# A hybrid decoder step on one core: moving one store and four PSUM copies between queues

## The chip, the core and the metric

The kernel runs on one core of one Trainium2 chip. The metric is the device time of one execution in microseconds; where several runs are shown, their median counts. The core has five engines with a queue each: PE (TensorE, matmuls; its weight loads are listed as PEld), DVE (VectorE), ACT (ScalarE), POOL (GpSimd) and SP (SyncE), which here issues most of the transfers. ACT's queue issues transfers too. An instruction that waits holds up whatever stands behind it on its engine.

## The reference

One layer of a decoder is computed in float32 for one prompt of 256 positions and for eight decoded sequences with one new token each, 264 columns in all. Cut to what matters here:

```python
def trunk_layer(x, attend, shift0, wkv0, lp):
    x = x + FFN_RES * swiglu(rmsnorm(x, n1), f1g, f1u, f1d)
    h = rmsnorm(x, nm)
    proj = h @ w_in
    q, k, v = ...                      # attention columns of proj
    o_att, k_buf, v_buf = attend(q, k, v, sinks)
    o_rwkv, shift, S = rwkv_time_mix(proj[..., ATT_COLS:], shift0, wkv0, ...)
    x = x + concat([o_att, o_rwkv]) @ w_out
    x = x + FFN_RES * swiglu(rmsnorm(x, n2), f2g, f2u, f2d)
    return x, k_buf, v_buf, S, shift

def rwkv_time_mix(proj, shift0, wkv0, ...):
    prev = concat([shift0[:, None], proj[:, :-1]], axis=1)
    xm = proj + mu * (prev - proj)     # r, k, v and three LoRA inputs are cut from xm
    ...
    def step(S, inp):                  # over the positions, for each of 16 heads of 64
        r_t, lw_t, k_t, v_t, kk_t, a_t = inp
        sa = einsum('bhij,bhj->bhi', S, -kk_t)
        S = (S * exp(lw_t)[:, :, None, :] + sa[..., None] * (kk_t * a_t)[:, :, None, :]
             + v_t[..., None] * k_t[:, :, None, :])
        return S, einsum('bhij,bhj->bhi', S, r_t)
    ...
    return out, proj[:, -1], S
```

The returned `proj[:, -1]` (the last projected row of the prompt and the row of each decoded token) is the shift state. It is one of the outputs.

## The kernel before

**Stages.** The first feed-forward block runs to about 780 us, the mixing stage (input projection, time mixing, attention, output projection) from there to about 1152 us, and the second feed-forward block to the end. All large matmuls go through `gemm` (lines 135 to 150 of the file): a weight block of 128x512 is loaded by SP into `raw`, split by ACT into `hi` (L132) and by DVE into `lo` (L59, a helper of all two-tensor operations), and each 128-column slice of it costs three matmuls (hi by hi, hi by lo, lo by hi) into a bank `acc` of PSUM. All matmuls that go through the helper `mm` have line 75; in `gemm` the name `big[0]` always holds the last matmul that was issued.

**The mixing stage.** `SEQ` lists the projected tiles: four batches `b`, then four `kv` tiles, then eight query tiles `q`. A batch has two pairs of heads (`BATCH = [2, 2, 2, 2]`), and for each pair three tiles are projected by `shifted`. `shifted` scales the tile (`pj`), and POOL copies its last nine columns to `shc` (L412); after the last of the 26 tiles `shc` holds the whole shift state.

**Tasks.** The work beside the projection is written as generators (`prep`, `chain`, `kvtask`, `attend`, `dec_scores`), advanced one step at a time by `tick` while `gemm` runs. This is the order in which the program is written down; a scheduler then puts the instructions of each engine into a list by their priorities and by a modelled time. `tc.high_priority()` lifts some of them, and `behind` ties an instruction in the scheduler to `big[0]`, without a semaphore on the chip.

**A batch's chain.** `chain(bt)` does, for the two pairs k = 0 and 1 of a batch: a triangular solve by DVE (30 steps of two operations, tiles `X`, `Xt` and `st`), whose inputs come back through DRAM by `Xt<-sa`; the second half of the inverse by small matmuls on `TT` and `W`, copied out by ACT (L600, L609); 16 matmuls for each pair, `m<-kr,TT`, into one PSUM bank each (`wus[k]`); from these banks the blocks `W[:, k]` (L622) and the two halves of `uv` (L626: half 0 by DVE, half 1 by ACT); then 24 matmuls for each pair on `W` (`m<-BT,W` and `m<-gm,W`), copied by L640 to `PT` and by DVE to `kr`; then the matmuls `m<-uv,BT` and `m<-gm,uv`; then the recurrence over the four chunks of 64 positions. L622 gives W's block of pair 0 to ACT and that of pair 1 to DVE:

```python
(A.copy, V.tensor_copy)[k % 2](W[:, k], v[:, 1:4, 0:64])
```

`W` is one tile of one buffer, filled by L600 and by L622 in turn. The tile pool tagged `m` has five PSUM banks for all these small products.

**The store of the shift state.** After the last batch has been spawned, L887 issues `A.dma_start(O["sh"], shc)` on ACT's queue: 117 KB, behind the copies of POOL into `shc`. Query tiles come later: for each, `win` projects it, DVE scales it into `ob[i]` (L62) and `attend` is spawned.

Of the kernel before, what the change touches and what calls it, by code (L numbers as in the profile page):

```python
# [26 lines left out]
BATCH = [2, 2, 2, 2]  # L27
# [20 lines left out]
def body(tc, I, O):  # L48
    nc = tc.nc
    V, A, G, TE, SP = nc.vector, nc.scalar, nc.gpsimd, nc.tensor, nc.sync  # L50
# [7 lines left out]
    def tt(e, out, a, b, op):  # L58
        return e.tensor_tensor(out=out, in0=a, in1=b, op=op)  # L59
# [14 lines left out]
    def mm(out, lhsT, rhs, start=True, stop=True, **k):  # L74
        return TE.matmul(out, lhsT, rhs, start=start, stop=stop, **k)  # L75

    def behind(i):
        tc.add_manual_dep(i.ins, big[0].ins.name, mybir.DependencyInfo(mybir.DependencyClass.NoSync, mybir.DependencyReason.SCHED_ONLY))
        return i
# [12 lines left out]
    def spawn(g):  # L92
        tasks.append(g)
        return g

    def pause(n):
        for _ in range(n):
            yield

    with ExitStack() as ctx:  # L100
# [14 lines left out]
        def tmp(shape=(P, T), dt=F32):  # L115
            pool, n = cur[0]
            return pool.tile(list(shape), dt, tag="t", bufs=n, name=uid("t"))
# [4 lines left out]
        def mp():  # L122
            return pp.tile([P, 512], F32, tag="m", bufs=NM, name=uid("m"))
# [42 lines left out]
        def vc(i):  # L166
            return vec[:, i:i + 1]
# [189 lines left out]
        def mixing_body(mx, n2, n3, XD, XR):  # L357
            def fix(shape, name):
                return mx.tile(list(shape), F32, name=name)

            def ring(shape, tag, bufs):
                return mx.tile(list(shape), F32, tag=tag, bufs=bufs, name=uid(tag))

            def load(src, shape):
                t = ring(shape, "ld", NLD)
                SP.dma_start(t, src)
                return t
# [6 lines left out]
            shc = fix((P, NSH, NB + 1), "shc")  # L374
# [24 lines left out]
            def win(t):  # L399
                ps = acc()  # L400
                gemm(ps, I["win"][t], n2.xs, tick)
                if not have[0]:
                    n2.rstd(rs)
                    have[0] = True
                return ps
# [137 lines left out]
            def newbatch(i):  # L543
                bt = Batch()
                n = BATCH[i]
                bt.i, bt.n, bt.left, bt.p0, bt.near = i, n, n, sum(BATCH[:i]), 0
                bt.KR, bt.bv = [None] * n, [None] * n
                bt.Gm = [[None, None] for _ in range(n)]
                bt.BT = [None] * n
                bt.UV = ring((P, 4, n, P), "uv", NUV)  # L550
                return bt

            def chain(bt):
# [27 lines left out]
                W, PT = ring((P, n, 3, 64), "W", 1), ring((P, n, 3, 64), "PT", 1)  # L581
# [37 lines left out]
                            mm(wus[k][r, c * P:c * P + P], TT[r, k * 4 + c, :], bt.KR[k][r, 0:3:2, c, :])  # L619
                for k in range(n):  # L620
                    v = wus[k].rearrange("p (c t) -> p c t", c=4)
                    (A.copy, V.tensor_copy)[k % 2](W[:, k], v[:, 1:4, 0:64])  # L622
                for k in range(n):
                    v = wus[k].rearrange("p (c t) -> p c t", c=4)
                    for h in range(2):
# [12 lines left out]
                for k in range(n):  # L638
                    v = pbs[k][:, :384].rearrange("p (c t) -> p c t", c=3)
# [104 lines left out]
            def softmax(s, mxv, sinks, n):  # L744
                nm, sm, es = (ring((P, 4), "st" + x, 6) for x in "abc")
                ts(V, nm[:, :n], mxv[:, :n], -1.0, ALU.mult)
                for j in range(n):
                    act(s[j], s[j], AF.Exp, bias=nm[:, j:j + 1], accum_out=sm[:, j:j + 1])
                w = n // len(sinks)
                for h, x in enumerate(sinks):  # L750
                    act(es[:, h * w:(h + 1) * w], nm[:, h * w:(h + 1) * w], AF.Exp, bias=x)
                tt(V, sm[:, :n], sm[:, :n], es[:, :n], ALU.add)
                V.reciprocal(sm[:, :n], sm[:, :n])
                for j in range(n):
                    if j < 2:
                        ts(V, s[j], s[j], sm[:, j:j + 1], ALU.mult)
                    else:
                        act(s[j], s[j], AF.Copy, scale=sm[:, j:j + 1])

            def attend(t, q):  # L760
                p = t // 4
                G.tensor_copy(qd[:, p, :, t % 4], q[:, NP:T])
                bs = [load(I["bias"][(2 * p + h) * 4 + t % 4], (P, 256)) for h in range(2)]
                yield
                spp = [mp(), mp()]
                for h in range(2):
                    mm(spp[h][:, 0:256], q[:, P:NP], kT[p][h][:, 0:NP])
                    mm(spp[h][:, 256:384], q[:, 0:P], kT[p][h][:, 0:P])
                sc = [(tmp((P, 256)), tmp((P, P))) for h in range(2)]
                mxv = ring((P, 4), "mxv", 6)  # L770
                for h, sps in enumerate(spp):
                    s1, s0 = sc[h]
                    head = (2 * p + h) * 4 + t % 4
                    for s, a, b, j in ((s1, sps[:, 0:256], bs[h], 0), (s0, sps[:, 256:384], bs[h][:, P:256], 1)):
                        V.tensor_tensor_reduce(out=s, in0=a, in1=b, op0=ALU.add, op1=ALU.max, scale=1.0,
                                               scalar=vc(VSK + head), accum_out=mxv[:, 2 * h + j:2 * h + j + 1])
                softmax([x for y in sc for x in y], mxv, [vc(VSK + (2 * p + h) * 4 + t % 4) for h in range(2)], 4)
                yield
                yield from pause(PW[4])
                for s1, s0 in sc:  # L780
                    tp = mp()
                    TE.transpose(tp[:, 0:P], s0, ident)  # L782
                    TE.transpose(tp[:, P:2 * P], s1[:, 0:P], ident)
                    TE.transpose(tp[:, 2 * P:3 * P], s1[:, P:256], ident)
                    A.copy(s1, tp[:, 0:256])
                    V.tensor_copy(s0, tp[:, 256:384])
                yield
                pt = sc
                op = mp()
                for h in range(2):  # L790
                    mm(op[:, h * 256:h * 256 + 256], Vt[p][:, 0, :], pt[h][0], True, False)
                    mm(op[:, h * 256 + P:h * 256 + 256], Vt[p][:, 1, :], pt[h][1], False, True)
                for h in range(2):
                    A.copy(q[HALF[h], :NP], op[HALF[h], h * 256:h * 256 + 256])
                mixed[8 + t] = q
# [80 lines left out]
            bat, att, bts, scores = [], [], [], []  # L876
            for kind, i in SEQ:
                if kind == "b":
                    bt = newbatch(i)
                    for k in range(BATCH[i]):  # L880
                        p = bt.p0 + k
                        x = [shifted(2 + 3 * p + j, tmp()) for j in range(3)]
                        spawn(prep(p, bt, k, *x))
                    bat.append(spawn(chain(bt)))
                    bts.append(bt)
                    if len(bat) == len(BATCH):
                        A.dma_start(O["sh"], shc)  # L887
                elif kind == "kv":
                    w, p = i // 2, i % 2
                    ps = win(LKV + i)  # L890
                    if w:
                        xs = (tmp(),)
                        with tc.high_priority():
                            tt(V, xs[0], ps[:, :T], rs, ALU.mult)
                    else:
                        xs = (kvb[2 * p], kvb[2 * p + 1])
                        kT[p] = xs
                        for h in range(2):
                            G.memset(xs[h][HALF[1 - h], :], 0.0)
                            with tc.high_priority():  # L900
                                tt(V, xs[h][HALF[h], :], ps[HALF[h], :T], rs[HALF[h], :], ALU.mult)
                    spawn(kvtask(w, p, xs))
                else:
                    ps = win(LKV + 4 + i)
                    q = ob[i]
                    with tc.high_priority():
                        stt(q, ps[:, :T], 0.125, rs, ALU.mult, ALU.mult)
                    att.append(spawn(attend(i, q)))
                    if i % 4 == 3:
                        scores.append(spawn(dec_scores(i // 4)))  # L910
                    if len(att) == 8:
                        att.append(spawn(dec_attend(list(att), scores)))
# [201 lines left out]
```

## Time and profile before

| | us |
|---|---|
| median of 3 runs | 1961.34 |
| lowest and highest | 1960.53, 1962.97 |
| the profiled execution, whole | 1958.83 |
| the profiled execution, its span | 1957.0 |
| PE idle in the stretch 780 to 1152 us | 6.16 |

The span goes from the first to the last instruction; the whole time has a little more at both ends. In what follows, a row of a timeline has the start (us from the span's start), the length, the engine, the line of the kernel, the operation and the tiles (written <- read), and in brackets how long the engine was idle before it and what released it. A row of a list of waits has the total us, the number and the longest. The chain of waits is the work that ended last, followed back from the last instruction. "ACTq" and "SPq" are DMA issues on those queues.

### The profile page before, as it was taken

To read this page: it belongs to the slowest core of one execution; us is meant where nothing else is said; L and a number is where in the kernel's file an instruction comes from. 1 tells how busy PE (TensorE), PEld (TensorE's weight loads), DVE (VectorE), ACT (ScalarE), POOL (GpSimd) and SP (SyncE) were. 2 spreads that over 40 slices of the span, in tenths; PEclk is the share of its full clock that TensorE was granted. 3 is DMA by queue.
4 is the path that set the end of the run, shared out by engine and by line. 5 is a ranking of instruction groups with operands and counts; after the bars stand their busy time and mean duration, and the time that the engine had idled before them with its cause. 6 is when DMAs were issued, how large, how long until landed. Compare 5 with 4: busy or idle time off the path is not lost.

```text
span 1957.0 us, 45229 instructions
## 1 busy us (share of the span) xinstructions
PE 1940.1 (99%) x17011; PEld 1922.1 (98%) x17011; DVE 1313.1 (67%) x2591; ACT 1036.4 (53%) x2069; POOL 264.1 (13%) x382
## 2 busy tenths in 40 slices
PE   9999999999999999999999999999999999999998
PEld 9999999999999999999889999999999999999998
DVE  5865555655556567799988766766666666666665
ACT  5644444444444456665556755654444444444445
POOL 0401001010010122232210000210101001010012
PEclk9999999999999999999999999999999999999999
DMA  7666666666656567555455455566666666666654
GB/s 241 178 194 194 186 194 196 184 189 178 188 183 185 184 194 230 165 162 153 136 151 167 137 157 185 176 187 188 191 189 193 188 194 191 191 195 183 195 182 148
DMA packets 218875, 357.26 MB, mean 183 GB/s; under 512 B 33552, under 2 KB 72352, under 8 KB 218656
## 3 DMA queue, kind: packets, MB, share of 16 engines
q1 hardware_dynamic: 212144, 345.76, 59.4%
q10 hardware_dynamic: 6512, 8.61, 1.4%
q8 instruction: 133, 2.18, 0.4%
q14 instruction: 86, 0.70, 0.1%
HBM read 346.67 MB, written 9.69 MB: 182 GB/s over the span
## 4 chain that ended last, share of the span: by engine, by line
PE 95%; DVE 3%; DMA 1%; issue 1%; ACT 1%; SPq 0%; DVEq 0%; POOL 0%; ACTq 0%
PE acc L75 87%; PE m L75 7%; DVE lo L59 1%; DVE Xt L59 0%; DVE st L59 0%; DMA Xt<-sa 0%; DMA x<-in_x 0%; DMA raw<-in_win 0%; DVE y L59 0%; SPq L564 0%; DVE gm L59 0%; ACT t L69 0%; DMA sa<-gm 0%; PE m L782 0%; ACT BT L521 0%
## 5 line engine op out<-in xcount | busy, mean ns | idle before, releaser
L59 DVE TENSOR_TENSOR lo<-raw,hi 128x512 fp32r<-128x512 f32 (+1 forms) x1288 | 874.5, 683 | 511.0 <-ACT hi L132 489.8
L132 ACT CAST hi<-raw 128x512 fp32r<-128x512 f32 (+1 forms) x1288 | 777.0, 606 | 822.0 <-PE acc L75 741.5
L75 PE MATMUL acc<-x,hi 128*128 128x264 f32 x5034 | 932.7, 286 | 2.2 <-DVE o L62 1.2
L75 PEld LDWEIGHTS acc<-x,hi 128*128 128x128 f32 x5034 | 781.4, 189 | 5.8 <-ACT hi L132 2.4
L75 PE MATMUL acc<-x,lo 128*128 128x264 f32 x2517 | 719.8, 286 | 0.5 <-DVE lo L59 0.5
L75 PE MATMUL acc<-h,hi 128*128 128x264 f32 x2752 | 495.0, 284 | 0.0
L75 PEld LDWEIGHTS acc<-x,lo 128*128 128x128 f32 x2517 | 475.5, 189 | 2.9 <-DVE lo L59 1.3
L75 PEld LDWEIGHTS acc<-h,hi 128*128 128x128 f32 x2752 | 424.4, 189 | 0.0
L75 PE MATMUL acc<-h,lo 128*128 128x264 f32 x1376 | 387.8, 284 | 0.0
L75 PEld LDWEIGHTS acc<-h,lo 128*128 128x128 f32 x1376 | 259.2, 189 | 0.0
L59 POOL TENSOR_TENSOR t<-t,t 128x264 f32<-128x264 f32 x74 | 80.3, 1085 | 1095.9 <-DVE t L59 949.7
L75 PE MATMUL acc<-y,hi 128*128 128x264 f32 x648 | 122.7, 284 | 0.0
L75 PE MATMUL acc<-o,hi 128*128 128x264 f32 x648 | 120.1, 284 | 0.0
L75 PE MATMUL acc<-kv,hi 128*128 128x264 f32 x582 | 109.2, 284 | 0.0
L75 PEld LDWEIGHTS acc<-y,hi 128*128 128x128 f32 x648 | 101.2, 189 | 0.1
L75 PEld LDWEIGHTS acc<-o,hi 128*128 128x128 f32 x648 | 100.1, 189 | 0.0
L62 DVE SCALAR_TENSOR_TENSOR x<-acc,x 128x264 f32<-128x264 f32 x192 | 81.2, 427 | 24.5 <-PE acc L75 23.6
L75 PE MATMUL acc<-y,lo 128*128 128x264 f32 x324 | 92.0, 284 | 0.0
L75 PE MATMUL acc<-o,lo 128*128 128x264 f32 x324 | 92.0, 284 | 0.0
L75 PEld LDWEIGHTS acc<-kv,hi 128*128 128x128 f32 x582 | 90.0, 189 | 0.0
L59 DVE TENSOR_TENSOR t<-acc,t 128x264 f32<-128x264 f32 x156 | 67.4, 432 | 32.8 <-PE acc L75 32.8
L75 PE MATMUL acc<-kv,lo 128*128 128x264 f32 x291 | 82.7, 284 | 0.0
(280 smaller groups left out, 1534.9 us busy)
## 6 DMA issues: line engine op xcount, KB each, us to landing
raw<-in_gu SPq DMA_DIRECT2D x688, 256.0 KB, 3.4
raw<-in_dn SPq DMA_DIRECT2D x224, 256.0 KB, 2.9
raw<-in_win SPq DMA_DIRECT2D x152, 256.0 KB, 3.4
raw<-in_dn SPq DMA_DIRECT2D x160, 192.0 KB, 2.7
raw<-in_wout SPq DMA_DIRECT2D x64, 256.0 KB, 3.3
xsp<-x ACTq DMA_DIRECT2D x16, 132.0 KB, 3.6
x<-xsp SPq DMA_DIRECT2D x16, 132.0 KB, 4.0
ld<-in_sT SPq DMA_DIRECT2D x16, 128.0 KB, 3.7
```

What stands on the lines that cost most here:

```text
L59: return e.tensor_tensor(out=out, in0=a, in1=b, op=op)
L62: return V.scalar_tensor_tensor(out=out, in0=a, scalar=s, in1=b, op0=op0, op1=op1)
L75: return TE.matmul(out, lhsT, rhs, start=start, stop=stop, **k)
L132: A.copy(hi[:, :w], raw[:, :w])
```

## The change

Two edits. L622 uses ACT for both pairs. The store of the shift state is taken out of the branch of the batches and issued after query tile 1 has been projected and its `attend` spawned; it is put through `behind`, so that the scheduler places it after the last matmul of that tile's projection. It stays on ACT's queue.

```diff
@@ -619,7 +619,7 @@
                 for k in range(n):
                     v = wus[k].rearrange("p (c t) -> p c t", c=4)
-                    (A.copy, V.tensor_copy)[k % 2](W[:, k], v[:, 1:4, 0:64])
+                    A.copy(W[:, k], v[:, 1:4, 0:64])
@@ -883,8 +883,6 @@
                     bat.append(spawn(chain(bt)))
                     bts.append(bt)
-                    if len(bat) == len(BATCH):
-                        A.dma_start(O["sh"], shc)
                 elif kind == "kv":
@@ -906,6 +904,8 @@
                     att.append(spawn(attend(i, q)))
+                    if i == 1:
+                        behind(A.dma_start(O["sh"], shc))
                     if i % 4 == 3:
```

## The prediction

> **What bounds the kernel now.** I read the page first, then the busy times by stage, then who PE waited for in the mixing stage, and only then the chain of waits and the rows of all engines around those waits.
>
> ```profile
> span 1957.0 us, 45229 instructions
> PE 1940.1 (99%) x17011; PEld 1922.1 (98%) x17011; DVE 1313.1 (67%) x2591; ACT 1036.4 (53%) x2069; POOL 264.1 (13%) x382
> 780.00:1152.00 372.00, 365.84 (x3924) 349.21 (x3923) 308.26 (x868) 235.70 (x622) 66.04 (x152) 1.00 0.54 152
> ```
>
> PE is the bound over the whole execution. The edit sits in the mixing stage, about 780 to 1152 us (third row: length of the stretch, then busy us of PE, PEld, DVE, ACT and POOL, granted clock, DMA share, GB/s). There PE is idle for 372.00 - 365.84 = 6.16 us. An edit that shortens no PE work, as this one, can give back about that much at most: 0.31% of the time. What PE waited for there, and what ACT waited for (total us, times, longest):
>
> ```profile
> PE m L75 <- ACT TT L609: 1.5, 1, 1.5
> PE m L75 <- DVE W L622: 1.3, 2, 0.9
> ...
> ACT hi L132 <- PE acc L75: 61.9, 62, 3.1
> ...
> ACT TT L609 <- POOL shc L412: 3.8, 1, 3.8
> ...
> ACT uv L626 <- DVE uv L626: 3.2, 1, 3.2
> ```
>
> The first two rows are the places that the edit touches: 1.5 + 1.3 = 2.8 us of PE. The question is whether PE keeps these 2.8 us or waits again a few instructions later. The row with shc is the store: L609 stands behind it in ACT's queue, and the store waits for the last copy into shc.
>
> **The store.** It is one DMA on ACT's queue. Here is its surrounding in time order (start, length, engine, line; idle time before it in brackets), in batch 1, the second of four:
>
> ```profile
> 950.62 0.19 DVE L59 TENSOR_TENSOR st<-X,Xt 128x30 f32<-128x30 f32 x1 [1.68 <-DMA Xt<-sa]
> 953.03 0.68 POOL L412 COPY shc<-pj 128x9 f32<-128x9 f32 x1 [4.38 <-DVE pj L59]
> 953.75 0.35 ACTq L887 DMA_DIRECT2D out_sh<-shc  x1
> 954.14 0.75 ACT L609 COPY TT<-m 32x256 f32<-32x256 f32 x2 [3.83 <-POOL shc L412]
> 954.55 2.35 PE L75 MATMUL m<-kr,TT 64*64 64x128 f32 x32 [1.46 <-ACT TT L609]
> 956.11 0.32 ACT L622 COPY W<-m 128x192 f32<-128x192 f32 x1
> 958.34 0.41 DVE L626 COPY uv<-m 64x256 f32<-64x256 f32 x1
> 958.49 0.33 PE L75 MATMUL m<-BT,W 64*64 64x64 f32 x4
> 959.39 0.34 DVE L622 COPY W<-m 128x192 f32<-128x192 f32 x1
> 959.66 0.41 DVE L626 COPY uv<-m 64x256 f32<-64x256 f32 x1
> 959.79 0.33 PE L75 MATMUL m<-BT,W 64*64 64x64 f32 x4 [0.38 <-DVE W L622]
> 960.10 0.37 ACT L626 COPY uv<-m 64x256 f32<-64x256 f32 x1
> 960.63 1.15 PE L75 MATMUL m<-uv,BT 128*64 128x64 f32 x32
> ```
>
> Without the store in front, ACT can do L609 3.83 us sooner, and PE starts the 32 matmuls m<-kr,TT 1.46 us sooner, at 953.09. In an unchanged order everything of PE behind them moves up by 1.46, and the matmuls on W start at 958.49 - 1.46 = 957.03. They need 0.91 us for each pair (958.49 to 959.40, the second start less its wait of 0.38), so they would end near 958.85. Next in PE's queue come the matmuls on uv, and uv's second pair is written by DVE and then ACT. What is late next is therefore DVE's uv, and DVE does not care for the store: from 950.62 to 959.66 it runs without a wait through the triangular solve of the next batch. The chain that ended last says the same. It does not pass through the store:
>
> ```profile
> 946.49 4.04 DMA Xt<-sa
> ...
> 958.42 0.33 DVE uv L626
> 958.75 0.60 DVE bk L59
> ...
> 959.47 0.28 DVE W L622
> ...
> 959.79 2.93 PE m L75 x88
> ```
>
> The chain lies on DVE before 959.79, and further back it goes to the transfer Xt<-sa. So in an unchanged order the store alone gives PE 1.46 us at 953 and takes it back at 959: **0** is the value I take for it alone. Its bounds are 0 and -1.46.
>
> At its new place the store comes behind the last matmul of query tile 1, by a tie for the scheduler only, with no semaphore on PE. shc has been complete since 953.71 (953.03 + 0.68), so it waits for nothing there. It costs ACT's queue the 0.35 of its row; the gap before the W copy of batch 2 (0.94, below) is larger. The transfer passes the small stores of keys and values on the same queue; none of them has a reader in the kernel:
>
> ```profile
> out_kp<-kv ACTq DMA_DIRECT2D x4, 32.0 KB, 3.3
> ...
> out_sh<-shc ACTq DMA_DIRECT2D x1, 117.0 KB
> ```
>
> Those are four stores each for kp and vp, and 117 KB beside a stage that moves 152 GB/s x 372 us = 56.5 MB. Value 0; if the cover of ACT's gap is gone, 0.35 on ACT.
>
> **The W copies.** Four copies (one in each batch) leave DVE and go to ACT:
>
> ```profile
> L622 ACT COPY W<-m x4: 319/319/319, 887.1 to 1070.1; 128x192 f32<-128x192 f32 x4
> L622 DVE COPY W<-m x4: 327/347/351, 888.3 to 1069.9; 128x192 f32<-128x192 f32 x4
> ```
>
> DVE sheds 4 x 0.347 = 1.39 us, ACT takes 4 x 0.319 = 1.28 us. The same bytes move, so PE's matmuls are unchanged.
>
> [...]
>
> *Batch 1.* W's second block would be ready on ACT by 956.11 + 0.64 = 956.75, before the 957.03 computed above, so the wait of 0.38 goes. DVE's second uv starts at 959.39 in place of 959.66, 0.27 sooner. ACT's uv follows it 0.44 later (959.66 to 960.10), so it ends near 959.39 + 0.44 + 0.37 = 960.20, and PE starts on uv at about 960.35 with a handoff of 0.15 as an estimate (959.79 less the end of the W copy, 959.73, is 0.06; a little more is left for ACT's queue). Against 960.63 that is **-0.28**. Here the edit as a whole removes 1.46 + 0.38 = 1.84 us of waits and gets 0.28.
>
> *Batch 2.* The same copies, at query tile 1:
>
> ```profile
> 1020.10 0.32 ACT L622 COPY W<-m 128x192 f32<-128x192 f32 x1 [0.94 <-PE m L75]
> ...
> 1023.59 0.37 ACT L626 COPY uv<-m 64x256 f32<-64x256 f32 x1 [3.17 <-DVE uv L626]
> 1023.88 0.35 DVE L622 COPY W<-m 128x192 f32<-128x192 f32 x1
> 1024.28 0.20 PEld L75 LDWEIGHTS m<-BT,W 64*64 64x64 f32 x4 [1.03 <-DVE W L622]
> 1024.62 0.37 ACT L626 COPY uv<-m 64x256 f32<-64x256 f32 x1
> 1025.13 1.15 PE L75 MATMUL m<-uv,BT 128*64 128x64 f32 x32
> ```
>
> ACT is idle for 3.17 us behind its first W copy, so the second costs nothing there. PE's W wait (0.89 on PE, 1.03 on the weight load) goes, and PE then waits for ACT's second uv, which ends at 1024.99: at once only 0.1 is gained. DVE, however, is 0.35 ahead from here on, and it holds the path to the next PE wait. I take the DVE copy's length, **-0.35**; bounds 0 and -0.89.
>
> *Batches 0 and 3.* PE does not wait for W there, so there is no wait to remove. In batch 3 ACT runs without a gap from its W copy to its second uv, and that uv is what PE's next matmuls need:
>
> ```profile
> 1070.12 0.32 ACT L622 COPY W<-m 128x192 f32<-128x192 f32 x1
> 1070.33 0.80 ACT L69 ACTIVATE t<-t,stb 128x256 f32<-128x256 f32 x2
> ...
> 1072.73 0.37 ACT L626 COPY uv<-m 64x256 f32<-64x256 f32 x1
> 1072.96 1.28 PE L75 MATMUL m<-uv,BT 128*64 128x64 f32 x31
> ```
>
> One more copy ahead of it makes it later by 0.21 (1070.12 to 1070.33, the step from one to the next) to 0.32: **+0.21**. In batch 0 I take 0: what else stands between is work that PE does anyhow.
>
> Behind an added ACT copy queue the casts hi<-raw, which feed every matmul. Their cover is the 61.9 us in which the casts themselves wait for PE to free a buffer (62 times, 1.0 us on average): 0.32 is inside that. Without this cover all 1.28 would be on PE.
>
> **Sum.** 0 - 0.28 - 0.35 + 0.21 = -0.42 us. The profiled execution took 1958.83 us, 1.83 more than its span of 1957.0, and the runs shown have a median of 1961.34, 2.51 above it. Span 1957.0 - 0.42 = 1956.6; on the median **1960.9**. Unknown is what a new list order does: the whole program is scheduled again behind the first moved copy at 887, and no row shows that. From the rows, its bounds are -6.16 (all PE idle of the stage) and, on the other side, the blocked queues below.
>
> **Rivals.** *All removed waits are kept.* The new order puts gemm matmuls between W and uv, or DVE's uv ahead of solve steps, so that nothing else becomes late: 1.46 + 1.27 (0.38 + 0.89), and DVE's 1.39 on its path to PE as well: -4.1, 1957.2 us. For it: the last chain lies on DVE at both places. Against: the DVE queue is without a gap there, and W copies are only two of its many steps.
>
> *Slower: ACT blocked behind DVE's uv.* In batch 2 ACT stood idle 3.17 us for DVE's uv, and the store's 3.83 us cost PE 1.46; so from 3.83 - 1.46 = 2.4 us of a blocked ACT on, each further us is one of PE. With both W copies early on ACT and uv late on DVE, ACT could stand before uv for 3.8 us in three more batches: 3 x 1.46 = 4.4, with no gain from the rest: 1965.7 us. For it: DVE is that late in batches 1 and 2. Against: the list of ACT's waits, quoted above, has that wait once in four batches.
>
> *It does nothing.* Both gains are taken back by the next DVE wait and batch 3's cost stays: 0 to +0.2, 1961.4 us.
>
> **How the numbers follow.** Changes within 0.2%, 3.9 us, can't be told from no change here. Forecast 0.45, nothing 0.15, all kept 0.20, blocked 0.20. The first two are inside the bound, the third is faster, the fourth slower: faster 0.2, same 0.6, slower 0.2. The likeliest is 1960.9, with its own range from -2.7 to +1.0 for the order, 1958.6 to 1962.3. The whole range reaches to the two others and slightly short of all PE idle: 1956.8 to 1965.7.
>
> **What would show it.** Right: no ACT wait for POOL shc at L609; PE's matmuls on TT start sooner behind the gemm of the last projected tile; no PE wait for DVE W; a new or longer PE wait for uv (ACT or DVE L626) in batches 1 and 2; PE idle of the stage between 5 and 6.2 us. Wrong: PE idle below 3 us (the gain was kept), or ACT waits of over 2.4 us in front of L626 with PE idle above 9 us. If the order of PE's gemm and batch matmuls is another one, the sum holds only by its bounds.

## The result, and the profile after

The changed kernel takes 1969.57 us (median of 6 runs, 1966.69 to 1974.05) against 1960.42 us for the kernel before (1959.19 to 1962.97, 6 runs): a ratio of 1.0054, 95% interval 1.0044 to 1.0064. It is slower by 9.15 us, where 1960.9 us was forecast, and it lies beyond the upper end of the range, 1965.7. The profiled execution took 1971.91 us, 1.8 more than its span.

From the page and from the busy times by stage of the changed kernel (PE, PEld, DVE, ACT, POOL, then granted clock, DMA share, GB/s):

```profile
span 1970.1 us, 45231 instructions
PE 1947.6 (99%) x17011; PEld 1929.0 (98%) x17011; DVE 1315.6 (67%) x2587; ACT 1040.2 (53%) x2075; POOL 263.3 (13%) x382
...
780.00:1152.00 372.00, 359.64 (x3849) 342.79 (x3847) 305.46 (x850) 235.00 (x612) 64.42 (x149) 0.99 0.53 150
```

The first thing to see is that PE is idle for 372.00 - 359.64 = 12.36 us in the mixing stage, where it was 6.16. The second is PE's busy total: as many matmuls as before take 7.5 us longer, and the granted clock of the stage is 0.99 where it was 1.00. Idle and clock together are the 13.1 us by which this span is longer: 6.2 us more of idle time, and the slices of 20 us that were granted less than full clock (a slice at 0.91 loses 9% of 20 us, 1.8 us; the kernel before has no slice below 1.00 between 780 and 1160 us):

```profile
960.00:980.00 20.00, 19.79 (x233) 18.45 (x234) 18.77 (x68) 10.20 (x28) 4.74 (x10) 0.91 0.41 112
1020.00:1040.00 20.00, 16.93 (x247) 15.67 (x247) 18.51 (x75) 5.67 (x14) 0.95 (x4) 0.91 0.36 101
1140.00:1160.00 20.00, 19.23 (x132) 18.66 (x131) 9.20 (x27) 6.53 (x19) 1.13 (x3) 0.83 0.36 110
```

1.8 + 1.8 + 3.4 = 7.0 us, so 6.2 + 7.0 = 13.2. This execution lies 2.3 us above the median of its kernel; the share of the clock differs from run to run: the mean granted clock of the six runs goes from 0.993 to 0.997.

What PE waited for (total us, times, longest) in the stage and up to 1215 us:

```profile
PE m L75 <- ACT W L622: 4.8, 2, 3.1
PE acc L75 <- DVE o L62: 2.6, 1, 2.6
PE m L75 <- ACT t L69: 1.4, 1, 1.4
```

The waits for ACT's TT (1.5) and for DVE's W (1.3) are gone, as the change intends. In their place PE waits 4.8 us for the W copies on ACT, and 1.4 us for an activation t on ACT, which is a new wait. The wait for the query eviction o (DVE's scaling of a finished query tile, which it reads from PSUM) has grown to 2.6 from the row of the kernel before:

```profile
PE acc L75 <- DVE o L62: 1.2, 1, 1.2
```

The rows of all engines around the first of these (start, length, engine, line; idle time before it in brackets) show what stands between the two W copies of batch 1:

```profile
954.03 1.96 PE L75 MATMUL m<-kr,TT 64*64 64x128 f32 x32
955.23 0.32 ACT L622 COPY W<-m 128x192 f32<-128x192 f32 x1 [2.00 <-PE m L75]
...
959.35 0.61 ACT L69 ACTIVATE t<-t,less,half 128x264 f32<-128x264 f32 x1 [3.80 <-DVE t L62]
...
959.86 0.30 ACT L622 COPY W<-m 128x192 f32<-128x192 f32 x1
960.21 0.33 PE L75 MATMUL m<-BT,W 64*64 64x64 f32 x4 [1.69 <-ACT W L622]
...
1026.71 0.37 ACT L626 COPY uv<-m 64x256 f32<-64x256 f32 x1 [5.28 <-DVE uv L626]
1027.10 0.32 ACT L622 COPY W<-m 128x192 f32<-128x192 f32 x1
1027.47 0.33 PE L75 MATMUL m<-BT,W 64*64 64x64 f32 x4 [3.07 <-ACT W L622]
```

The second copy does not follow the first. In batch 1 (954 to 960 us) an activation that waits 3.80 us for DVE stands in between, in batch 2 a uv copy that waits 5.28 us for DVE. That looks like the whole cause: ACT blocked behind DVE, as in the slower rival. The experiments say that it is not.

### The profile page after: what moved, and what is told of

Its sections match the earlier page's. It is cut to its first block, busy times and chain, and to the rows that moved or that the text cites. A ratio compares the mean times of both kernels' runs of the same rounds, so it can differ in the third digit from the quotient of the medians.

```text
span 1970.1 us, 45231 instructions
## 1 busy us (share of the span) xinstructions
PE 1947.6 (99%) x17011; PEld 1929.0 (98%) x17011; DVE 1315.6 (67%) x2587; ACT 1040.2 (53%) x2075; POOL 263.3 (13%) x382
## 4 chain that ended last, share of the span: by engine, by line
PE 94%; DVE 2%; DMA 1%; ACT 1%; issue 1%; SPq 0%; ACTq 0%; DVEq 0%; POOL 0%
PE acc L75 86%; PE m L75 7%; DVE lo L59 1%; DMA Xt<-sa 0%; DMA sa<-gm 0%; DVE st L59 0%; DVE Xt L59 0%; DMA x<-in_xT 0%; DMA ld<-in_cv 0%; DVE y L59 0%; ACT t L69 0%; SPq L564 0%; DVE t L716 0%; DVE gm L59 0%; ACT L69 0%
## 5 line engine op out<-in xcount | busy, mean ns | idle before, releaser
L75 PE MATMUL acc<-x,hi 128*128 128x264 f32 x5034 | 933.0, 286 | 4.0 <-DVE o L62 2.6
L75 PEld LDWEIGHTS acc<-x,hi 128*128 128x128 f32 x5034 | 782.9, 189 | 7.6 <-issue 3.1
L75 PE MATMUL acc<-x,lo 128*128 128x264 f32 x2517 | 721.8, 287 | 1.0 <-DVE lo L59 1.0
L75 PE MATMUL acc<-h,hi 128*128 128x264 f32 x2752 | 495.0, 284 | 0.0
L75 PEld LDWEIGHTS acc<-x,lo 128*128 128x128 f32 x2517 | 476.5, 189 | 3.7 <-DVE lo L59 1.8
L75 PEld LDWEIGHTS acc<-h,hi 128*128 128x128 f32 x2752 | 424.4, 189 | 0.0
L75 PE MATMUL acc<-h,lo 128*128 128x264 f32 x1376 | 387.9, 284 | 0.0
L75 PEld LDWEIGHTS acc<-h,lo 128*128 128x128 f32 x1376 | 259.2, 189 | 0.0
L75 PE MATMUL acc<-y,hi 128*128 128x264 f32 x648 | 122.7, 284 | 0.0
L75 PE MATMUL acc<-o,hi 128*128 128x264 f32 x648 | 120.1, 284 | 0.0
L75 PE MATMUL acc<-kv,hi 128*128 128x264 f32 x582 | 109.2, 284 | 0.0
L75 PEld LDWEIGHTS acc<-y,hi 128*128 128x128 f32 x648 | 101.2, 189 | 0.1
L75 PEld LDWEIGHTS acc<-o,hi 128*128 128x128 f32 x648 | 100.1, 189 | 0.0
L75 PE MATMUL acc<-o,lo 128*128 128x264 f32 x324 | 92.0, 284 | 0.0
L75 PE MATMUL acc<-y,lo 128*128 128x264 f32 x324 | 92.0, 284 | 0.0
L75 PEld LDWEIGHTS acc<-kv,hi 128*128 128x128 f32 x582 | 90.0, 189 | 0.0
L75 PE MATMUL acc<-kv,lo 128*128 128x264 f32 x291 | 82.7, 284 | 0.0
```

## The experiments

Each run is set against runs of the kernel before on the same chip. The edits are shown shortened. In the kernels with held lists the line numbers are 12 higher (L75 is L87 there).

**Which edit.** First each edit alone:

```
e1_wcopy   -  (A.copy, V.tensor_copy)[k % 2](W[:, k], v[:, 1:4, 0:64])
           +  A.copy(W[:, k], v[:, 1:4, 0:64])
e2_store   -  if len(bat) == len(BATCH): A.dma_start(O["sh"], shc)
           +  if i == 1: behind(A.dma_start(O["sh"], shc))
```

> The W edit alone: L622 on ACT for both pairs, the store where it was before. Theory A (ACT's queue order: the second W copy stands behind an ACT instruction that waits for DVE, L69 in batch 1 and L626 in batch 2, and PE idles for it): nearly the whole loss is here, 1967 to 1971 us, PE waits for ACT W L622 of about 3 us and 1.7 us less what the store's block of ACT covers. Theory B (the moved store is what hurts, by another order behind it): within 2 us of the kernel before, and no PE wait for ACT W over 1 us.

> The store edit alone: the store behind query tile 1, L622 on ACT and DVE in turn as before. Theory A: within 2 us of the kernel before (1958.5 to 1962.5), the wait of ACT TT for POOL shc gone, and a PE wait for DVE W or uv in batch 1 that has grown by about what was saved. Theory B: 1967 us or more.

The W copies alone: 1969.1 us, ratio 1.0050 [1.0035, 1.0065]. The store alone: 1961.8 us, 1.0009 [0.9999, 1.0018]. So the loss comes with the copies. The store's own row shows how its gain is lost; who PE waited for in e2_store:

```profile
PE m L75 <- DVE W L622: 2.3, 1, 2.3
```

The 1.46 us for TT are gone, and the wait for DVE's W in batch 1 has grown to 2.3: a little more than the 1.46 + 0.38 of before. DVE was on the path behind the store all along.

**Is it the place in ACT's queue?** Two kernels let the second W copy come ahead of what blocked it. In e3_tie_uv the uv copies on ACT are tied behind the second W copy; in e5_tie_pool POOL also does the activation that stood in between:

```
e3_tie_uv    +  wk = A.copy(W[:, k], v[:, 1:4, 0:64])
             +  tc.add_manual_dep(uv_copy.ins, wk.ins.name, NoSync SCHED_ONLY)
e5_tie_pool  -  act(a, a, AF.Identity, scale=half[:, p:p+1], bias=less[:, p:p+1])
             +  ts(G, a, a, half[:, p:p+1], ALU.mult, less[:, p:p+1], ALU.add)
```

> The changed kernel with ACT's two uv copies of a batch tied, for the scheduler alone, behind the second W copy. This changes the order only in batch 2, where uv stood between the W copies; in batch 1 the activation L69 still stands between them. Theory A: the PE wait of 3.07 us for ACT W in batch 2 goes and with it the stretch at half clock behind it; that of 1.69 us in batch 1 stays: 3 to 5 us less than the changed kernel, 1964.5 to 1966.5. Rival C (not the queue but DVE's lag: PE only waits for uv instead): the same as the changed kernel within 1.5 us.

> As the run before it, and the activation t<-t,less,half of L69, which waits for DVE, is done by POOL, so that both W copies of every batch stand next to each other in ACT's queue. Theory A: no PE wait for ACT W in any batch, no half clock in batches 1 and 2: 1958.5 to 1963, near the kernel before. Rival C: PE waits for uv as long as it did for W, and the time is that of the changed kernel.

e3_tie_uv: 1968.8 us, 1.0051 [1.0036, 1.0066]. e5_tie_pool: 1968.47 us, 1.0048 [1.0033, 1.0063]. Who PE waited for in e5_tie_pool:

```profile
PE acc L75 <- DVE o L62: 2.6, 1, 2.6
PE m L75 <- DVE uv L626: 2.3, 3, 1.5
```

No wait for W is left, and the time is that of the change within its interval. Taking the visible wait away moved it to uv. This speaks against the blocked ACT queue as the cause. It does not settle it, since the scheduler made the lists of these two kernels anew as well; e7_after_lists and e8_queue below do.

**Is it the clock?** In the changed kernel PE runs at half clock behind its two waits for W: the granted clock is 0.50 from 961 to 964 us, behind the wait of 1.69 us, and from 1029 to 1032 us, behind that of 3.07 us. e4_fill keeps PE busy in these two with idle matmuls of 128 columns (8 in batch 1, 18 in batch 2) into the bank of the pair, ahead of its W matmuls; they are work on top of the changed kernel's:

```
e4_fill  +  if k: for _ in range((0, 8, 18, 0)[bt.i]): mm(pbs[k][:, 0:P], ones, ones)
```

> The changed kernel with idle matmuls of 128 columns on PE between the matmuls on W of pair 0 and of pair 1: 8 in batch 1, 18 in batch 2 (they write a bank that is written anew right behind). They fill PE's two waits for ACT W in part (about 0.9 and 2.0 us of 1.7 and 3.1). Theory F (PE's clock is halved for some 3.5 us behind a wait that is long enough, and each such stretch costs about 1.7 us): no half clock behind these two places, 1966 to 1968 us. If the clock has another cause: half clock stays, and the time is that of the changed kernel or up to 1 us more.

1968.0 us, 1.0044 [1.0028, 1.0059]: 1.6 us below the changed kernel, with intervals that overlap. In its profile the slices at 960 and 1020 us are back at full clock, and one at 1080 to 1100, in which PE was never idle, is at 0.91. So the loss is there at nearly full clock too (0.998 in this execution). The run does not size the share of the clock, because its waits are other ones as well: the wait for t is gone, and there is one of 2.1 us for ACT's TT.

**The lists.** What is left is that every engine's list of instructions behind the first moved copy is made anew. e6_held has both edits, but holds the list of every engine in the mixing stage to that of e2_store; only the four copies change engine, and each stands directly behind the first W copy of its batch on ACT. e7_after_lists is the opposite: the store edit, the copies left on DVE, and all lists held to those of the changed kernel. e8_queue is e6_held with the second W copy where the changed kernel has it in ACT's queue, behind the instruction that waits for DVE.

```
+  def hold(tc):                      # called behind the body
+      for row in ORDER.values():     # one written-out list for each engine
+          for a, b in zip(row, row[1:]):
+              tc.add_manual_dep(by[b], a, NoSync SCHED_ONLY)
```

> Both edits, but every engine's list in the mixing stage is held, by ties for the scheduler, to the list of the kernel that has the store edit alone (whose lists are those of the kernel before but for the store). The second W copy stands directly behind the first in ACT's list, in all four batches. Theory D (the lists that the scheduler makes anew from batch 1 on are what costs, not the copies on ACT): 1959 to 1962 us, as the prediction's sum has it for an unchanged order. Theory E (a DVE that is late makes PE wait whatever the order): 1965 us or more.

> The store edit, the W copies of pair 1 on DVE as before, but every engine's list in the mixing stage held to that of the changed kernel; the DVE copy stands directly ahead of the second uv copy, as before. Theory D: the loss is here too, though no copy has changed its engine: 1966 to 1970 us. Theory A (ACT's queue alone): 1959 to 1963 us.

> Both edits, lists held to those of the kernel with the store edit alone, but the second W copy put where the changed kernel has it in ACT's list: behind L69 in batches 0 and 1, behind the first uv copy in batch 2. Theory A: 1964 us or more, with PE waits for ACT W of 1.5 to 3 us. Theory D: between 1960 and 1963.5: the two waits of PE for W move by about 1 us and the rest of the lists is the old one.

e6_held: 1959.38 us, 0.9999 [0.9990, 1.0008]. e7_after_lists: 1971.17 us, 1.0056 [1.0040, 1.0073]. e8_queue: 1958.42 us, 0.9998 [0.9989, 1.0007]. (e7_after_lists came out 1.2 us above what was expected of it, e8_queue 1.6 us below.) This settles the main question. Both edits in the old order cost nothing that can be told, and the new order without any copy on another engine has the whole loss. In the old order even the blocked place on ACT costs nothing that can be told: ACT stands there for 3.28 and 3.12 us, where it was 3.80 and 5.28 in the changed kernel, and PE waits 2.1 us for W. e6_held's stage and PE's waits:

```profile
780.00:1152.00 372.00, 367.07 (x3933) 350.59 (x3932) 308.00 (x866) 237.62 (x628) 66.92 (x155) 1.00 0.54 152
```

```profile
PE acc L87 <- DVE o L74: 1.2, 1, 1.2
...
PE m L87 <- ACT uv L638: 0.8, 3, 0.3
```

PE is idle for 372.00 - 367.07 = 4.93 us, 1.2 less than before. Both W waits are gone; what is left is three short waits for ACT's uv, the next late instruction that the prediction named.

**Which copy.** The edit in one batch alone, batch 1 or batch 2:

```
f1_batch1  +  (A.copy, (V.tensor_copy, A.copy)[bt.i == 1])[k % 2](W[:, k], v[:, 1:4, 0:64])
f2_batch2  +  (A.copy, (V.tensor_copy, A.copy)[bt.i == 2])[k % 2](W[:, k], v[:, 1:4, 0:64])
```

> The W edit in batch 1 alone, the store where it was, lists free. The scheduler then makes other lists from this copy on, with 214 differing lines on PE. If batch 1's copy is what tips the lists: 1966 to 1970 us, the whole loss. If each batch's copy gives its part: about a third of it, 1962 to 1964 us.

> The W edit in batch 2 alone, the store where it was, lists free; other lists arise only from this copy on (139 differing lines on PE, from 1020 us on). If the loss of the changed kernel arises before that (its query tile 1 was already 6.7 us late): within 3 us of the kernel before, 1957 to 1963. If it arises with this batch's queue: 1965 us or more.

f1_batch1: 1967.73 us, 1.0038 [1.0027, 1.0050]. f2_batch2: 1960.02 us, 0.9997 [0.9988, 1.0007]. One copy of 0.32 us in batch 1 brings most of the loss. The lists of both differ widely from those of before (on PE in 214 lines for f1_batch1 and in 139 for f2_batch2), so it is not that any new list is slower: this one is.

**Which engine's list.** g2_pe holds PE's list alone to the old one, g1_dve DVE's alone; the others are made anew.

> Both edits; PE's list alone is held to that of the kernel with the store edit alone, all others are made anew (DVE's differs from the held one in 158 lines). If PE's order carries the loss (a block of 12 gemm matmuls is put off from batch 1's chain to later): 1959 to 1962 us. If it is DVE's order (the end of batch 2's solve ahead of the evictions of the query tiles): 1965 us or more.

> Both edits; DVE's list in the mixing stage alone is held to that of e2_store (with the four moved copies taken out), the lists of the other engines are made anew behind it, and PE's then differs from the held one in 4 lines. If the loss sits in DVE's new list: as e6_held, 1959.4, ratio 0.999 to 1.001, the query evictions o at their old times and PE's wait for o 1.2 us. If it sits in PE's or ACT's new list: 1964 or more, ratio above 1.002. If the clock falls whatever the lists are: 1967 or more with 20 us windows of the mixing stage at 0.9 or less.

g2_pe: 1967.12 us, 1.0036 [1.0023, 1.0049]. g1_dve: 1960.7 us, 1.0003 [0.9994, 1.0012]. With PE in its old order the loss stays; with DVE in its old order it is gone. PE's waits, first in g2_pe, then in g1_dve:

```profile
PE acc L87 <- DVE o L74: 2.6, 1, 2.6
PE m L87 <- ACT W L634: 1.7, 1, 1.7
PE m L87 <- ACT t L81: 1.5, 1, 1.5
```

```profile
PE m L87 <- ACT W L634: 2.7, 2, 1.8
PE acc L87 <- DVE o L74: 1.2, 1, 1.2
```

PE waits longer for W in g1_dve than in g2_pe, and g1_dve is the faster one by 6 us. The rows that go with the loss are those for o and for ACT's t: o is 1.2 us in g1_dve, and t is not there. Of all kernels here, those with the loss wait 1.9 to 3.0 us for o, those without it 1.2. With DVE's list held the scheduler also gives PE nearly its old list back (4 lines differ), so g1_dve alone does not say through which engine the loss is made.

**Which stretch of DVE's list.** The list was cut at two places where old and new have the same instructions behind them. i3_new_1280 has the new order in the first stretch (from batch 1's uv copies to just ahead of the first query eviction) and every other list old. j4_mid has it in the second stretch only (the end of the solve and the first query evictions), with PE's list old. j1_new_1354 has it in both, with PE's list old. In the last two the other engines' lists are made anew. All three have both edits. All of DVE's new list with every other list old was not run.

> Both edits, all lists of the mixing stage held to those of e2_store but for one stretch of DVE's, from batch 1's uv copies to the step ahead of the first query eviction, which has the changed kernel's order (solve steps of the next batch ahead of recurrence steps and of the key and value evictions). If this stretch carries the loss: 1964 to 1968, ratio above 1.002, the first key and value eviction 2 us later. If it does not: as e6_held, 1959.4, ratio 0.999 to 1.001.

> Both edits, PE's list held to that of e2_store, DVE's too but for the next stretch, which has the changed kernel's order: the end of the solve (X, PT, TT transposes) stands ahead of the first query evictions o. If this carries the loss: PE waits 2.6 us for o instead of 1.2, 1964 to 1968, ratio above 1.002. If it does not: 1959 to 1962, ratio below 1.001.

> Both edits, PE's list held to that of e2_store, DVE's in the changed kernel's order over both stretches and in the old order behind them. If the two stretches carry the loss: as g2_pe, 1966 to 1968, ratio above 1.003. If it is made behind them, in the evictions of the later query tiles: 1959 to 1962, ratio below 1.001; about 1963 if half of it is.

i3_new_1280: 1959.67 us, 0.9999 [0.9990, 1.0008]. j4_mid: 1965.72 us, 1.0033 [1.0020, 1.0045]. j1_new_1354: 1968.27 us, 1.0042 [1.0029, 1.0054]. The second stretch, with what the scheduler makes of the other engines' lists behind it, costs 6.2 us. DVE's rows there, first in the kernel before, then in j4_mid:

```profile
994.96 0.43 DVE L580 STREAM_TRANSPOSE X<-Xt 128x256 f32<-128x256 f32 x1
995.33 0.39 DVE L62 SCALAR_TENSOR_TENSOR o<-acc,rs 128x264 f32<-128x264 f32 x1
...
996.58 0.41 DVE L59 TENSOR_TENSOR PT<-X,unit 128x256 f32<-128x256 f32 x1
...
998.22 0.84 DVE L588 STREAM_TRANSPOSE TT<-PT 32x256 f32<-32x256 f32 x2
```

```profile
989.92 0.43 DVE L592 STREAM_TRANSPOSE X<-Xt 128x256 f32<-128x256 f32 x1
...
990.92 0.41 DVE L71 TENSOR_TENSOR PT<-X,unit 128x256 f32<-128x256 f32 x1
...
993.52 0.42 DVE L597 STREAM_TRANSPOSE TT<-PT 128x256 f32<-128x256 f32 x1
993.87 0.84 DVE L600 STREAM_TRANSPOSE TT<-PT 32x256 f32<-32x256 f32 x2
...
995.70 0.42 DVE L74 SCALAR_TENSOR_TENSOR o<-acc,rs 128x264 f32<-128x264 f32 x1
```

In the old list the eviction of the first query tile, which frees a PSUM buffer for PE (it waits 1.24 us for it), stands directly behind the transpose X. In the new one PT and the transposes to TT stand ahead of it: 0.41 + 0.42 + 0.84 = 1.67 us. (The other rows between X and o in the second view, among them a reciprocal of 1.79 us, stand ahead of o in the old list too.) What this does to PE in j4_mid (rows of PE that waited):

```profile
996.27 0.48 PE L87 MATMUL acc<-x,hi 128*128 128x264 f32 x2 [2.96 <-DVE o L74]
...
1019.86 0.39 PE L87 MATMUL acc<-x,lo 128*128 128x264 f32 x1 [2.54 <-DVE lo L71]
...
1054.20 0.92 PE L87 MATMUL m<-kv,o 128*128 128x256 f32 x4 [1.47 <-ACT t L81]
```

(2.96 - 1.2) + 2.54 + 1.47 = 5.8 us; 1.2 is the same wait in e6_held, which has neither of the other two. The first difference, 1.8, is about the 1.67 us of DVE work put ahead of the eviction. PE's idle time in the stage agrees, and every 20 us slice of it has full clock, so in this execution no part of the loss is clock:

```profile
780.00:1152.00 372.00, 361.14 (x3890) 344.64 (x3888) 304.41 (x856) 236.57 (x615) 61.85 (x149) 1.00 0.53 151
```

372.00 - 361.14 = 10.86 us, 5.9 more than e6_held. The wait at 1019.86 comes out of DVE's queue too. The cast lo that PE wants stands behind the first steps of the last batch's solve, and the first of them waits for a transfer:

```profile
1017.89 0.19 DVE L71 TENSOR_TENSOR st<-X,Xt 128x30 f32<-128x30 f32 x1 [3.37 <-DMA out_vp<-t]
...
1019.12 0.68 DVE L71 TENSOR_TENSOR lo<-raw,hi 128x512 fp32r<-128x512 f32 x1
```

The named transfer, a small store, is only the one that ended last by the profile; in the kernel before, and in the changed one, the same step waits for Xt<-sa, and it starts at 1014.98 and at 1019.91 us. This wait of 2.54 us belongs to j4_mid and j1_new_1354 (2.45), where the new stretch meets the old order behind it. The changed kernel and g2_pe, which have all of DVE's new list, wait no more than 0.8 us for any lo. So j4_mid loses about as much as the changed kernel, but in part by another wait.

The third wait is not made on DVE. It is for the second t<-m,eps on ACT, whose list was made anew. Rows of ACT ahead of it, first in the kernel before, then in j4_mid:

```profile
1044.02 0.51 ACT L69 ACTIVATE t<-t,sta 128x256 f32<-128x256 f32 x1
...
1046.28 1.28 ACT L69 ACT_TABLE_LOAD   x1
1047.57 0.85 ACT L69 ACTIVATE t<-m,eps 128x264 f32<-128x264 f32 x2
```

```profile
1047.03 1.28 ACT L81 ACT_TABLE_LOAD   x1
1048.33 0.48 ACT L81 ACTIVATE t<-m,eps 128x264 f32<-128x264 f32 x1
1048.83 1.28 ACT L81 ACT_TABLE_LOAD   x1
1050.12 0.51 ACT L81 ACTIVATE t<-t,sta 128x256 f32<-128x256 f32 x1
...
1052.38 1.28 ACT L81 ACT_TABLE_LOAD   x1
1053.67 0.48 ACT L81 ACTIVATE t<-m,eps 128x264 f32<-128x264 f32 x1
```

Wherever ACT goes, in these rows, from the activations on sta to t<-m,eps or back, there is an ACT_TABLE_LOAD, a table load, between. In the old list both t<-m,eps stand behind the activations on sta, with one table load between. In the new one the first of them stands ahead of these: two more table loads of 1.28 us each. The trace of the changed kernel has 18 table loads, that of the kernel before 16. The nine kernels here with 18 all have a PE wait for ACT's t, of 0.6 to 1.5 us, and all have the loss; no kernel with 16 has that wait. But e4_fill has 16 and the loss all the same, so this order can be a part of the loss and not the whole. No run has DVE's new stretch with ACT's list old. In g1_dve, where only DVE's list is held, ACT's is back to 16 loads: the scheduler makes this order of ACT only together with DVE's new one.

## Why the prediction was wrong

*The sum.* Its terms were 0 for the store, -0.28, -0.35, +0.21 and 0 for the copies, -0.42 us together, for an unchanged order. e6_held measures just that: 1959.38 us, a ratio of 0.9999 whose interval, about ±1.8 us, holds the -0.42. "So in an unchanged order the store alone gives PE 1.46 us at 953 and takes it back at 959" is what e2_store's rows show, and its interval leaves out the other bound of -1.46 but can't tell 0 from a loss of 3.5 us. "PE then waits for ACT's second uv" is in e6_held's rows, with 0.3 us a time. The waits of the old order were in the main read rightly.

*The step that failed* is the one that set the sum equal to the change: "Unknown is what a new list order does: the whole program is scheduled again behind the first moved copy at 887, and no row shows that." It was named, and then priced at nothing for the likeliest case. The lists did change, one copy in batch 1 being enough, and the new ones cost 9 to 11 us, not 0: 1971.17 us in e7_after_lists (ratio 1.0056), which has moved no copy to another engine, against 1959.38 in e6_held, which has moved all four and kept the order. In the changed kernel's profile 6.2 us of this are idle PE. The prediction looked only at instructions next to the moved ones. Part of the loss is made 40 to 96 us later, at an eviction o (2.60 us at 999.69, 1.4 more than before) and at an activation (1.38 at 1055.54), which the diff does not touch.

*The bounds.* "From the rows, its bounds are -6.16 (all PE idle of the stage) and, on the other side, the blocked queues below." The slower end thus came from a rival about two queues, 4.4 us, and had no term for a worse order. A start for that was in the profile of before: PE already waits 1.24 us for the eviction o there, so DVE work put ahead of it delays PE directly, as the 1.67 us in j4_mid did.

*The slower rival* had the right sign for another reason. "ACT waits of over 2.4 us in front of L626 with PE idle above 9 us" came true, with 5.28 us in front of uv and 12.36 us of idle PE, and would have passed for its proof. e8_queue has W blocked at the same place, if for a shorter time, and loses nothing; e5_tie_pool has no W wait and loses all. That sign was not specific: a wrong order shows the same rows.

*W's place.* "W's second block would be ready on ACT by 956.11 + 0.64 = 956.75" took for granted that the two copies are neighbours. The second one started at 959.86. In the kernel before, too, an activation (L69, at 958.34) stands between the first W copy and the uv copy on ACT and waits 1.91 us for DVE; the rows that the prediction quotes leave it out. The step was wrong, and by e8_queue's ratio of 0.9998 it cost nothing that can be told.

*The rest of the loss.* Idle time and clock can be told apart by the mean granted clock that is listed for every run. It is 0.9953 on average over the six runs of the changed kernel, 0.9966 over the five of j4_mid, and 0.9970 over the 21 runs of the kernel before that stand beside e6_held. As an estimate from these, 0.0017 x 1960 = 3.3 us of the 9.15 are clock in the changed kernel and 0.8 of the 6.2 in j4_mid; the rest, about 6 us and 5, is idle PE, which agrees with the 6.2 and 5.9 of the profiles. Which instruction makes which part was shown only for the 1.8 us at o. The two W waits of the changed kernel (4.8 us, where TT and W were 2.8) and the table loads were not taken away one by one in its own order, and the new order behind the second stretch was not run by itself. Why the scheduler preferred this order was not tried either.

## What to carry to other kernels

Where a scheduler orders the program, an edit of one instruction has two prices: its own, which the rows give, and that of the new lists behind it, which they don't; only the range can hold the second, on both sides. Measure the two apart by holding every list to the old one, and then hold one engine at a time; look also at what the other engines' lists do then, for they follow. Here four runs (e6_held, e7_after_lists, g1_dve, g2_pe) led from a total to DVE's list and what follows from it. An order can also cost instructions: count the table loads on ACT before and after (16 and 18 here, 1.28 us each). A large wait in the new profile right at the edit is no proof: take it away and see whether the time follows.

## What the runs showed of the hardware

In the changed kernel's profiled execution the granted clock falls to one half three times between 780 and 1160 us. By windows of 1 us it stays there for about 3.4 us (from 960.6 us on), 3.4 us (from 1028.9) and 6.8 us (from 1151.8), and these stretches are the 7.0 us of clock found in the slices above. Around the wait of 1.69 us the windows are (the number ahead of DMA share and GB/s is the clock):

```profile
959.00:960.00 1.00, 0.00 (x0) 0.00 (x0) 1.00 (x4) 0.65 (x2) 0.63 (x1) 1.00 0.74 154
960.00:961.00 1.00, 0.79 (x20) 0.79 (x22) 1.00 (x4) 0.95 (x3) 0.94 (x2) 0.81 0.91 264
961.00:962.00 1.00, 1.00 (x22) 0.88 (x20) 1.00 (x5) 1.00 (x4) 0.90 (x3) 0.50 0.35 119
...
963.00:964.00 1.00, 1.00 (x25) 1.00 (x24) 1.00 (x5) 0.14 (x1) 0.92 (x2) 0.50 0.16 59
964.00:965.00 1.00, 1.00 (x29) 0.93 (x25) 1.00 (x4) 0.00 (x0) 0.19 (x2) 0.98 0.69 143
```

The row left out has 0.50 as well. From 960 to 965 us the rows lose 0.19 + 0.50 + 0.50 + 0.50 + 0.02 = 1.71 us of full clock, which is 3.4 us at one half. The clock falls behind this wait and not in it: it is 1.00 from 959 to 960 us and 0.50 from 961 to 964. PE is busy without a break there, at half speed: 31 matmuls `m<-uv,BT` take 2.26 us at 961.38, where the kernel before needs 1.15 us for 32. So the wait of 1.69 us is followed here by a loss of another 1.71. Not every wait is: half clock followed those of 1.69 and 3.07 us in the changed kernel, while behind one of 2.96 us in j4_mid the clock stayed at 1.00, and e2_store's slice from 1080 to 1100 us, without any idle time, was granted 0.91:

```profile
1080.00:1100.00 20.00, 20.00 (x157) 18.89 (x157) 11.58 (x45) 11.75 (x37) 0.48 (x2) 0.91 0.45 123
```

What sets it off stays open, and no length of wait that does so can be read from these runs; e4_fill, which filled the two gaps at the W copies, has one such slice (0.91, 1080 to 1100 us) at another place.

A table load on ACT took 1.28 us on average in the kernel before and in the changed one, and 1.28 us in each of the rows of j4_mid above. How many there are depends here on the order of ACT's list: 16 in the kernel before, 18 in the changed one, and e6_held, with both edits in the old order, has 2073 instructions on ACT where the changed kernel has 2075.
